# Adding up the squares of two norms on GpSimd instead of VectorE, in a two-layer transformer trunk

## The chip, the core and the metric

The kernel runs on one core of a Trainium2 chip. The core's engines work beside each other: TensorE (PE in the profile; its weight loads are PEld), VectorE (DVE), ScalarE (ACT), GpSimd (POOL) and SyncE (SP), which here only issues DMAs. Each engine takes its instructions in a fixed order, and semaphores hold an instruction until what it reads is there. The metric is the device time of one execution in microseconds (us). Three executions of the kernel before took 1200.5, 1200.5 and 1201.09 us; the median is 1200.5 us.

## What is computed

The reference runs two layers over 512 tokens of width 1024, in float32, with a memory of 256 tokens beside them:

```python
mem_n = rms_norm(mem, mem_norm_g)
for l in range(2):
    h = rms_norm(x, mix_norm_g[l])
    x = x + (mixer_attn_rglru(h, ...) if l == 0 else pool_mixer(h, od_pool_w[0], od_scale[0]))
    x = x + memory_xattn(rms_norm(x, xattn_norm_g[l]), mem_n, ...)
    x = x + sq_relu_mlp(rms_norm(x, mlp_norm_g[l]), mlp_w1[l], mlp_w2[l])
```

`rms_norm` multiplies x by `rsqrt(mean(x*x) + 1e-6)` and by a gain; the mean runs over the 1024 features of a token. `pool_mixer`, the mixer of the second layer, takes four groups of 256 features; for each it forms the mean over the last 2, 4, 8 or 16 tokens less the token itself, multiplies by a 256x256 matrix, scales, and the result is added to x. So two norms lie around the pooling mixer: the mixer's own norm, and the norm of the cross attention that follows it.

## The kernel before

**Layout.** x lies in SBUF transposed, as eight tiles of 128 features x 512 tokens (`self.x[0]` to `self.x[7]`; in the profile they are halves of the tiles x_85 to x_88). Tokens run along a row. A token's sum of squares is therefore a sum over eight tiles and then over 128 partitions. `square_tile` squares a tile on ScalarE into a fresh tile `sq` (the method A, line 264), and adds it to the first norm tile's `sq`, which is the accumulator (the method `tt`, line 274, on VectorE): seven adds of 128x512 for a norm. When all eight are in, `stats` lets TensorE form the column sums (line 379, tile misc), VectorE scales them (tile m_4 for the norm ahead of the mixer, m_5 for the one behind it), and GpSimd raises them to the power -1/2 (the method `G`, line 296, tile r). For the norm ahead of the mixer TensorE then spreads r over the partitions (line 677) and ScalarE stores it as R.

**Matmuls.** Each float32 operand is split into a high and a low part, and each product is three matmuls: high by high, high by low and low by high (`mm3`, line 366). A weight block arrives as a 512 KB tile `raw`; ScalarE writes its high part `wh`, and VectorE subtracts to get the low part `wl` (128x1024). The same split gives `xh` and `xl` for x times the gain of the norm.

**The stage around the change.** At the end of the first layer's MLP (`mlp(0, ...)`), VectorE adds the last results to x, and the squares of the mixer's norm follow. TensorE goes on with the first group of keys of the second layer's memory (`kv_group(1, 0, ...)`), then with the pooling matmuls, then with the other three groups of `kv_group`, and then with the queries of the cross attention, whose input is x after the mixer, as `xh` and `xl`. Beside these matmuls VectorE works through the pooling: for each of the eight x tiles `z` (matmul result times R, out of PSUM), window sums `zs` (for two groups a running sum `zc`), `df`, the update of x, and then `xl` and the add of the squares for the next norm.

**Order.** A planner in Python writes all engines' instruction lists. It keeps a model of the time at which each engine is free (`book`), lets each piece of work ask for an engine with a due time (the table `DUE`), and gives the engine to the earliest due among those whose inputs the model has ready. For an add on VectorE the model books 0.00104 us for each element of a row and 0.065 us more (0.60 us for 512). For an operation on GpSimd that is not a power it books `0.00215 * n + 0.2`, which is 1.30 us for 512. The chip then runs the lists in that order, whatever the real times are.

Of the kernel before, what the change touches and what calls it, by code (L numbers as in the profile page):

```python
# [9 lines left out]
ALU = mybir.AluOpType  # L10
# [16 lines left out]
V_MEM, V_MIX, V_XA, V_MLP = 0, 8, 24, 40  # L27
# [111 lines left out]
class Trunk:  # L139
# [422 lines left out]
                    self.tick()  # L562


    def new_norm(self, gcol, bc, forms=False, first=False):
        self.nid += 1
        return dict(first=first, id=self.nid, g=gcol, bc=bc, h=[None] * 8, l=[None] * 8, n=0, acc=None,
                    forms={} if forms else None)

    def norm_tile(self, N, k):  # L570
# [18 lines left out]
    def square_tile(self, N, k):  # L589
        sq = self.slot("sq")  # L590
        yield from self.A(sq, self.x[k], AF.Square)
        if N["acc"] is None:
            N["acc"] = sq
        else:
            yield from self.tt(N["acc"], N["acc"], sq, ALU.add)
        N["n"] += 1
        if N["n"] == 8:
            if N["first"]:
                self.spawn(self.stats(N), self.blk)
            else:  # L600
                self.spawn(self.stats(N), self.blk + DUE["stats"], DUE["stats_d"])
# [910 lines left out]
    def run(self):  # L1512
        self.start()
        self.mixer()
        kv0 = self.new_kv()
        for g in range(4):
            self.kv_group(0, g, kv0)
        n1 = self.new_norm(V_XA, False)
        self.gemm_t(self.y_op, lambda m, ps: self.update(m, ps, n1))
        n2 = self.new_norm(V_MLP, True, True)  # L1520
        self.xattn(0, n1, kv0, n2)
        n3 = self.new_norm(V_MIX + 8, True, first=True)
        self.mlp(0, n2, n3)
        kv1 = self.new_kv()
        self.kv_group(1, 0, kv1)
        n4 = self.new_norm(V_XA + 8, False)
        self.pool_mix(n3, n4)
        for g in range(1, 4):
            self.kv_group(1, g, kv1)
        n5 = self.new_norm(V_MLP + 8, True, True)  # L1530
        self.xattn(1, n4, kv1, n5)
        self.mlp(1, n5, None)
        self.drain()
# [77 lines left out]
```

## Time and profile before

| what | value |
|---|---|
| median of three executions | 1200.5 us |
| the profiled execution, its own time | 1200.98 us |
| its span on the core | 1199.2 us |
| TensorE busy | 1184.4 us |
| VectorE busy | 933.0 us |
| ScalarE busy | 668.5 us |
| GpSimd busy | 151.4 us |
| mean clock granted to TensorE | 0.998 of full speed |

The span runs from the first to the last instruction on the core; what the execution takes beyond it, 1.8 us here, lies around it. A busy TensorE is not a TensorE at its peak, since matmuls overlap: successive 512-column matmuls start about 0.23 us apart, though each is shown 0.39 us long. A wait is shown as the idle time in front of an instruction, with the instruction that ended it.

### The profile page before, as it was taken

The page shows a single profiled execution, that of the slowest core. Times are in us where ns is not written, and L with a number is a line of the kernel's source. Part 1 is how long each engine was busy: PE and PEld are TensorE (multiplying, and loading weights), DVE is VectorE, ACT ScalarE, POOL GpSimd, SP SyncE. Part 2 cuts the span into 40 slices and gives each one's busy share as a digit, 9 for nine tenths or more (in the row PEclk, how much of TensorE's full clock was granted, in tenths as well). Part 3 has the DMA queues.
Part 4 walks back from the last instruction along what each step waited for, and adds up shares of the span by engine and source line. Part 5 has one row for each costly group of instructions (what it writes and reads, how often), then busy time and mean ns, then how long its engine had stood idle before and what let it go on. Part 6 is the DMA issues. An engine that isn't in the chain of part 4 may idle for free.

```text
span 1199.2 us, 20004 instructions
## 1 busy us (share of the span) xinstructions
PE 1184.4 (99%) x7984; PEld 1091.8 (91%) x7984; DVE 933.0 (78%) x1419; ACT 668.5 (56%) x965; POOL 151.4 (13%) x180
## 2 busy tenths in 40 slices
PE   9999999999999999999999999999999999999998
PEld 6887888888889999999999987788899999999998
DVE  7959886555559977969969999856599779599697
ACT  6487774345456735646546657344477356465462
POOL 0110010010101121111112010001011211111110
PEclk9999999999999999999999999999999999999999
DMA  9233353322447699899899654424476998999984
GB/s 365 79 132 101 122 178 119 97 91 77 88 98 190 175 250 236 213 259 236 215 242 292 182 175 140 136 77 83 101 193 171 250 237 215 250 242 212 245 211 106
DMA packets 61293, 212.22 MB, mean 177 GB/s; under 512 B 6928, under 2 KB 7440, under 8 KB 61200
## 3 DMA queue, kind: packets, MB, share of 16 engines
q1 hardware_dynamic: 41472, 141.68, 33.9%
q0 software_dynamic: 19584, 69.21, 31.7%
q8 instruction: 62, 1.02, 0.3%
q14 instruction: 31, 0.25, 0.1%
q10 hardware_dynamic: 144, 0.05, 0.0%
HBM read 206.73 MB, written 4.19 MB: 176 GB/s over the span
## 4 chain that ended last, share of the span: by engine, by line
PE 89%; DVE 7%; ACT 2%; issue 1%; DMA 0%; SPq 0%; DVEq 0%; ACTq 0%
PE acc L366 55%; PE misc L366 32%; DVE wl L274 2%; PE misc L373 1%; PE misc L379 1%; DVE x L274 1%; DVE xl L274 0%; DVE p L274 0%; DVE fl L274 0%; DVE hs L274 0%; ACT a L264 0%; DVE zc L274 0%; DVE sq L274 0%; DVE zs L274 0%; DMA raw<-wpack 0%
## 5 line engine op out<-in xcount | busy, mean ns | idle before, releaser
L264 ACT ACTIVATE wh<-raw 128x1024 fp32r<-128x1024 f32 (+1 forms) x321 | 334.1, 1050 | 309.4 <-PE acc L366 130.0
L274 DVE TENSOR_TENSOR wl<-raw,wh 128x1024 fp32r<-128x1024 f32 (+1 forms) x321 | 387.5, 1213 | 136.8 <-ACT wh L264 133.2
L415 POOL DMA_DIRECT2D raw<-wpack x128 | 111.3, 872 | 627.7 <-DVE wl L274 320.4
L366 PE MATMUL misc<-fl,wh 128*128 128x256 f32 x448 | 127.0, 283 | 1.1 <-DVE fl L274 1.1
L366 PE MATMUL acc<-fl,wh 128*128 128x256 f32 x448 | 126.9, 283 | 0.5 <-DVE x L274 0.5
L366 PE MATMUL misc<-fh,wh 128*128 128x256 f32 x448 | 126.8, 283 | 0.0
L366 PE MATMUL misc<-fh,wl 128*128 128x256 f32 x448 | 126.8, 283 | 0.0
L366 PE MATMUL acc<-fh,wh 128*128 128x256 f32 x448 | 126.8, 283 | 0.0
L366 PE MATMUL acc<-fh,wl 128*128 128x256 f32 x448 | 126.8, 283 | 0.0
L366 PEld LDWEIGHTS misc<-fl,wh 128*128 128x128 f32 x448 | 86.0, 192 | 1.5 <-DVE fl L274 1.5
L366 PEld LDWEIGHTS acc<-fl,wh 128*128 128x128 f32 x448 | 86.0, 192 | 0.7 <-DVE x L274 0.7
L366 PEld LDWEIGHTS acc<-fh,wh 128*128 128x128 f32 x448 | 86.0, 192 | 0.0
L366 PEld LDWEIGHTS acc<-fh,wl 128*128 128x128 f32 x448 | 86.0, 192 | 0.0
L366 PEld LDWEIGHTS misc<-fh,wl 128*128 128x128 f32 x448 | 86.0, 192 | 0.0
L366 PEld LDWEIGHTS misc<-fh,wh 128*128 128x128 f32 x448 | 86.0, 192 | 0.0
L366 PE MATMUL acc<-xh,wh 128*128 128x512 f32 x208 | 82.7, 398 | 2.7 <-ACT xh L264 1.7
L366 PE MATMUL acc<-xl,wh 128*128 128x512 f32 x208 | 82.7, 398 | 0.9 <-DVE xl L274 0.8
L366 PE MATMUL acc<-xh,wl 128*128 128x512 f32 x208 | 82.2, 395 | 1.4 <-DVE wl L274 1.4
L366 PE MATMUL acc<-oh,wh 128*128 128x512 f32 x160 | 62.7, 392 | 0.7 <-ACT oh L264 0.7
L366 PE MATMUL acc<-oh,wl 128*128 128x512 f32 x160 | 62.8, 392 | 0.0
L366 PE MATMUL acc<-ol,wh 128*128 128x512 f32 x160 | 62.5, 391 | 0.2 <-DVE ol L274 0.2
L366 PE MATMUL acc<-wl,mh 128*128 128x512 f32 x128 | 50.7, 396 | 1.1 <-DVE wl L274 1.1
(290 smaller groups left out, 3217.5 us busy)
## 6 DMA issues: line engine op xcount, KB each, us to landing
raw<-wpack SPq DMA_DIRECT2D x253, 512.0 KB, 4.8
raw<-wpack POOLq DMA_DIRECT2D x128, 512.0 KB, 7.3
x<-xT SPq DMA_DIRECT2D x8, 256.0 KB, 5.1
outT<-x SPq DMA_DIRECT2D x6, 256.0 KB, 2.2
raw<-wpack SPq DMA_DIRECT2D x4, 256.0 KB, 4.6
memr<-memT SPq DMA_DIRECT2D x4, 256.0 KB, 3.7
spill<-mh SPq DMA_DIRECT2D x4, 256.0 KB, 2.0
spill<-ml SPq DMA_DIRECT2D x4, 256.0 KB, 2.2
```

What stands on the lines that cost most here:

```text
L264: self.nc.scalar.activation(out, in_, func, **kw)
L274: getattr(self.nc.vector, fn)(out, *args, **kw)
L366: self.nc.tensor.matmul(out, a, b, start=start and i == 0, stop=stop and i == 2, skip_group_check=shared)
L373: self.nc.tensor.transpose(out, in_, self.ident)
L379: self.nc.tensor.matmul(ps[:, t:t + 1], sq[:, t * 128:t * 128 + 128], self.one, start=True, stop=True)
L415: self.nc.gpsimd.dma_start(out=raw, in_=self.ins["wpack"][b], accum_op=ALU.add)
```

## The change

`new_norm` takes a flag `gp`. In a norm that has it, the seven adds of `square_tile` are issued on GpSimd (through `G`) instead of VectorE (through `tt`). The two norms around the pooling mixer get the flag: `n3` ahead of it and `n4` behind it. The squares stay on ScalarE, and the other four norms stay as they were.

```diff
--- before.py
+++ after.py
@@ -562,9 +562,9 @@
                     self.tick()
 
 
-    def new_norm(self, gcol, bc, forms=False, first=False):
+    def new_norm(self, gcol, bc, forms=False, first=False, gp=False):
         self.nid += 1
-        return dict(first=first, id=self.nid, g=gcol, bc=bc, h=[None] * 8, l=[None] * 8, n=0, acc=None,
+        return dict(first=first, gp=gp, id=self.nid, g=gcol, bc=bc, h=[None] * 8, l=[None] * 8, n=0, acc=None,
                     forms={} if forms else None)
 
     def norm_tile(self, N, k):
@@ -591,6 +591,8 @@
         yield from self.A(sq, self.x[k], AF.Square)
         if N["acc"] is None:
             N["acc"] = sq
+        elif N["gp"]:
+            yield from self.G(N["acc"], N["acc"], sq, ALU.add)
         else:
             yield from self.tt(N["acc"], N["acc"], sq, ALU.add)
         N["n"] += 1
@@ -1519,11 +1521,11 @@
         self.gemm_t(self.y_op, lambda m, ps: self.update(m, ps, n1))
         n2 = self.new_norm(V_MLP, True, True)
         self.xattn(0, n1, kv0, n2)
-        n3 = self.new_norm(V_MIX + 8, True, first=True)
+        n3 = self.new_norm(V_MIX + 8, True, first=True, gp=True)
         self.mlp(0, n2, n3)
         kv1 = self.new_kv()
         self.kv_group(1, 0, kv1)
-        n4 = self.new_norm(V_XA + 8, False)
+        n4 = self.new_norm(V_XA + 8, False, gp=True)
         self.pool_mix(n3, n4)
         for g in range(1, 4):
             self.kv_group(1, g, kv1)
```

Since the planner sees other bookings, it also writes some rows in another order. Three places are shown. First, VectorE at the end of the first layer's MLP, before (aN and acc are MLP results that are added to x; x_85 to x_88 hold x):

```order
L274 TENSOR_TENSOR x_88<-x_88,aN 128x2x256
L274 TENSOR_TENSOR sq<-sq 128x512
L274 TENSOR_TENSOR x_87<-x_87,aN 128x2x256
L274 TENSOR_TENSOR x_88<-x_88,aN 128x2x256
L274 TENSOR_TENSOR x_87<-acc_76,x_87 128x2x256
L274 TENSOR_TENSOR wl<-raw,wh 128x1024
L274 TENSOR_TENSOR sq<-sq 128x512 x2
L274 TENSOR_TENSOR x_86<-acc_77,x_86 128x2x256
L274 TENSOR_TENSOR x_88<-acc_78,x_88 128x2x256
L274 TENSOR_TENSOR wl<-raw,wh 128x1024
L274 TENSOR_TENSOR sq<-sq 128x512 x2
L274 TENSOR_TENSOR wl<-raw,wh 128x1024
```

and after the change:

```order
L274 TENSOR_TENSOR x_88<-x_88,aN 128x2x256
L274 TENSOR_TENSOR x_87<-x_87,aN 128x2x256
L274 TENSOR_TENSOR x_88<-x_88,aN 128x2x256
L274 TENSOR_TENSOR x_87<-acc_76,x_87 128x2x256
L274 TENSOR_TENSOR wl<-raw,wh 128x1024
L274 TENSOR_TENSOR x_86<-acc_77,x_86 128x2x256
L274 TENSOR_TENSOR x_88<-acc_78,x_88 128x2x256
L274 TENSOR_TENSOR wl<-raw,wh 128x1024 x3
L274 SCALAR_TENSOR_TENSOR xl<-x_85,vec,xh 128x512 x2
```

The adds `sq<-sq` are gone, seven of them up to the first `xl`; the three weight conversions `wl` now follow each other, and the rest keeps its order.

Second, VectorE at the end of the pooling, from the first `xl` of x_88 to the second, which is the last tile that the queries need. Before:

```order
L274 SCALAR_TENSOR_TENSOR xl<-x_88,vec,xh 128x512
L274 TENSOR_TENSOR zs<-zc 128x496
L274 TENSOR_TENSOR sq<-sq 128x512
L274 TENSOR_TENSOR zs<-zs,cst 128x16
L274 TENSOR_TENSOR wl<-raw,wh 128x1024
L274 SCALAR_TENSOR_TENSOR df<-zs,z 128x512
L274 TENSOR_TENSOR sq<-sq 128x512
L274 SCALAR_TENSOR_TENSOR x_88<-df,vec,x_88 128x512
L274 TENSOR_TENSOR wl<-raw,wh 128x1024
L274 SCALAR_TENSOR_TENSOR xl<-x_88,vec,xh 128x512
```

and after the change:

```order
L274 SCALAR_TENSOR_TENSOR xl<-x_88,vec,xh 128x512
L274 SCALAR_TENSOR_TENSOR zc<-cst,z 128x512
L274 TENSOR_TENSOR wl<-raw,wh 128x1024
L274 TENSOR_TENSOR zs<-zc 128x496
L274 TENSOR_TENSOR wl<-raw,wh 128x1024
L274 TENSOR_TENSOR zs<-zs,cst 128x16
L274 SCALAR_TENSOR_TENSOR df<-zs,z 128x512
L274 TENSOR_TENSOR wl<-raw,wh 128x1024
L274 SCALAR_TENSOR_TENSOR x_88<-df,vec,x_88 128x512
L274 SCALAR_TENSOR_TENSOR xl<-x_88,vec,xh 128x512
```

Two adds are gone here, and the running sum `zc` with the weight conversion behind it comes after the first `xl` instead of ahead of it. From the end of the MLP to this last `xl` VectorE has the same 29 weight conversions in both, and 12 instructions fewer after the change: the seven adds of n3 and five of n4. The other two adds of n4 stood behind this place.

Third, GpSimd's list between the MLP and the queries (r_4 and r_5 are the powers of the two norms, xrk those of the memory's keys, xqs those of the queries). Before:

```order
L415 DMA raw<-wpack 128x1024 x2
L296 TENSOR_TENSOR r_4_7327<-m_4_7326,cst 128x4
L296 TENSOR_TENSOR xrk<-xvv,cst 128x2 x4
L296 TENSOR_TENSOR r_5_8023<-m_5_8022,cst 128x4
L296 TENSOR_TENSOR xqs<-xqv,cst 128x4 x2
```

and after the change:

```order
L415 DMA raw<-wpack 128x1024 x2
L296 TENSOR_TENSOR sq<-sq 128x512 x7
L296 TENSOR_TENSOR r_4_7333<-m_4_7332,cst 128x4
L296 TENSOR_TENSOR xrk<-xvv,cst 128x2 x4
L296 TENSOR_TENSOR sq<-sq 128x512 x7
L296 TENSOR_TENSOR r_5_8008<-m_5_8007,cst 128x4
```

The seven adds of n3 stand in front of r_4 and of the xrk, and the seven of n4 in front of r_5. On TensorE the column sums of n3 move back by one matmul, and in the pooling the accumulator banks change places.

## Rows read from the trace of the kernel before

**Rows 1.** The page's part 1: busy microseconds, share of the span and instructions of each engine
```profile
PE 1184.4 (99%) x7984; PEld 1091.8 (91%) x7984; DVE 933.0 (78%) x1419; ACT 668.5 (56%) x965; POOL 151.4 (13%) x180
```

**Rows 2.** Windows, all engines: stretch, its length, busy (xinstructions), clock, DMA share, GB/s
```profile
680.00:690.00 10.00, 9.10 (x56) 7.68 (x56) 9.79 (x15) 9.30 (x16) 0.00 (x0) 1.00 0.40 118
...
735.00:745.00 10.00, 9.78 (x43) 7.77 (x42) 9.97 (x15) 6.13 (x10) 0.00 (x0) 1.00 0.43 147
...
755.00:766.00 11.00, 9.23 (x40) 7.08 (x38) 11.00 (x15) 4.72 (x7) 0.00 (x0) 1.00 0.53 181
767.00:771.00 4.00, 4.00 (x12) 3.19 (x11) 3.06 (x5) 2.35 (x4) 0.00 (x0) 0.59 0.73 247
```

**Rows 3.** Waits of PE, 670 to 800 us: total, times, longest
```profile
PE acc L366 <- DVE wl L274: 2.5, 4, 1.4
PE acc L366 <- ACT xh L264: 1.7, 1, 1.7
PE acc L366 <- DVE xl L274: 0.5, 1, 0.5
```

**Rows 4.** Timeline of PE, end of the pooling mixer: start, us, instruction, idle before
```profile
744.85 0.39 PE L366 MATMUL acc<-xh,wh 128*128 128x512 f32 x1
745.08 0.39 PE L366 MATMUL acc<-xl,wh 128*128 128x512 f32 x1
746.88 0.50 PE L366 MATMUL acc<-xh,wl 128*128 128x512 f32 x1 [1.42 <-DVE wl L274]
...
763.34 0.39 PE L366 MATMUL acc<-xh,wl 128*128 128x512 f32 x1
765.38 0.50 PE L366 MATMUL acc<-xh,wh 128*128 128x512 f32 x1 [1.66 <-ACT xh L264]
766.43 0.50 PE L366 MATMUL acc<-xl,wh 128*128 128x512 f32 x1 [0.54 <-DVE xl L274]
...
768.52 0.63 PE L366 MATMUL acc<-xh,wl 128*128 128x512 f32 x1
768.95 0.63 PE L366 MATMUL acc<-xh,wh 128*128 128x512 f32 x1
```

**Rows 5.** Timeline of DVE, in the same columns, around both norms
```profile
681.06 0.69 DVE L274 TENSOR_TENSOR sq<-sq 128x512 f32<-128x512 f32 x1
681.66 1.29 DVE L274 TENSOR_TENSOR x<-x,aN 128x512 f32<-128x512 f32 x2
...
687.19 1.22 DVE L274 TENSOR_TENSOR wl<-raw,wh 128x1024 fp32r<-128x1024 f32 x1
...
765.62 0.75 DVE L274 SCALAR_TENSOR_TENSOR xl<-x,vec,xh 128x512 fp32r<-128x512 f32 x1
```

**Rows 6.** The tile sq: form, count, duration ns min/median/max, first and last start
```profile
L274 DVE TENSOR_TENSOR sq<-sq x42: 681/684/694, 9.3 to 900.9; 128x512 f32<-128x512 f32 x42
```

**Rows 7.** Timeline of DVE, two weight conversions early in the program
```profile
149.68 1.22 DVE L274 TENSOR_TENSOR wl<-raw,wh 128x1024 fp32r<-128x1024 f32 x1
...
151.81 2.36 DVE L274 TENSOR_TENSOR wl<-raw,wh 128x1024 fp32r<-128x1024 f32 x2
```

**Rows 8.** Timeline of POOL (GpSimd), small powers of 128x2 values
```profile
142.52 0.69 POOL L296 TENSOR_TENSOR m_r<-m_m,cst 128x2 f32<-128x2 f32 x1 [26.84 <-DVE m_m L274]
...
149.94 1.52 POOL L296 TENSOR_TENSOR xrk<-xvv,cst 128x2 f32<-128x2 f32 x1 [6.42 <-DVE xvv L274]
152.06 1.52 POOL L296 TENSOR_TENSOR xrk<-xvv,cst 128x2 f32<-128x2 f32 x1 [0.61 <-DVE xvv L274]
```

**Rows 9.** Groups of POOL instructions by form: count, busy us, mean ns
```profile
L1081 POOL MEMSET pth<- 128x128 f32 x4 | 0.8, 204 | 51.7 <-PE acc L366 51.7
...
L1602 POOL MEMSET const-float32-0.0<- 128x1 f32 x1 | 0.1, 98 | 0.2 <-issue 0.2
```

**Rows 10.** Timeline of PE, column sums of the first norm
```profile
693.82 0.95 PE L379 MATMUL misc<-cst,sq 128*128 128x1 f32 x8
```

## The prediction

> **What bounds the kernel now.** I began with the busy times by engine: TensorE is busy for 1184.4 of 1199.2 us and GpSimd for 151.4 [rows 1]. So a change that leaves the matmuls alone can only act where TensorE waits, and GpSimd as a whole has room. Next I cut the stretch from the end of the MLP to the queries into windows, since a mean over the program says nothing of this stage. Here VectorE is the full engine: it is busy for 9.79 of 10 us at 680 to 690, 9.97 of 10 at 735 to 745, and 11.00 of 11 at 755 to 766 [rows 2]. The list of TensorE's waits for 670 to 800 us says what this costs: four waits for a `wl`, 2.5 us in all, one of 1.7 us for an `xh`, and one of 0.5 us for an `xl` [rows 3]. The timeline of TensorE shows them: 1.42 us at 746.88 for a weight conversion, then 1.66 us and 0.54 us at 765.38 and 766.43, where it wants the last `xh` and `xl` of x behind the pooling [rows 4]. The `xh` is ScalarE's, but its input is the update of x on VectorE. So in this stage the time is set by when VectorE gets to its last `xl`, at 765.62 [rows 5].
>
> The waits cost more than their idle time. After the one of 1.42 us the start of the next matmul lies 1.80 us behind the last, where 0.23 us is the usual step: 0.15 us more than the idle time [rows 4]. For six waits that is 0.9 us. And at 767 to 771 the granted clock is 0.59 of full speed [rows 2]; within that stretch matmuls start 0.43 us apart, the step at 1.2 GHz instead of 2.4 [rows 4], just behind the longest waits. Over 4 us that is 4 x 0.41 = 1.6 us. All in all VectorE's lateness costs 4.7 + 0.9 + 1.6 = 7.2 us here, and that is the most that the change can win.
>
> **What VectorE gains.** One add of squares takes 684 ns at the median [rows 6], but the next instruction starts 0.60 us after it (681.06 to 681.66) [rows 5], so an add removed is worth 0.60 us. Up to the last `xl` there are 12 fewer: 7.2 us. If that were all, VectorE would come 7.2 us earlier to where TensorE waited 2.2 us after having already lost some 3 us upstream, and nearly all of the 7.2 us lost would come back.
>
> **What GpSimd takes, and what it does to VectorE.** No row shows an add of 128x512 on GpSimd, so its time is bounded. From below: a write of 128 elements takes 204 ns and one of a single element 98 ns [rows 9], so 0.83 ns an element, and 512 elements of one stream take 0.43 us. From above: an add has two reads and a write, 1.28 us if all three go one after the other; nothing makes it cheaper than one stream. The small operations of the same kind need 0.69 us for two elements [rows 8], but these are powers, so a part of this is computing. With a start-up of some 0.2 us the planner's own booking of 1.30 us lies inside, and I take 1.3 us for an add.
>
> That would be harmless on an idle engine, were it not for how the two engines meet. A power of 128x2 takes GpSimd 0.69 us at 142.52, but 1.52 us at 149.94 and at 152.06 [rows 8]. In both of the latter VectorE was in the middle of a `wl`, a subtraction with both inputs in SBUF: one from 149.68 to 150.90, the other the first of two from 151.81, which ends at about 153.03 [rows 7]. GpSimd's instructions end at 151.46 and 153.58, both 0.55 us behind the end of that `wl`. So GpSimd did not get its inputs until VectorE's two-input instruction was over, and in the second case it got in between two that followed each other closely. The two engines exclude each other on such reads, and the order is by who comes first. If VectorE holds GpSimd up, an add that GpSimd has begun should hold up VectorE's next two-input instruction, for as long as it reads. These rows can't show that, since two elements are read in no time; 512 are not.
>
> The Trainium skill says so in "SBUF — State Buffer", section "Who interferes with whom": a VectorE instruction with two SBUF inputs contends with a GpSimd instruction that reads SBUF, and whichever begins second is blocked for the whole of the other. The trace agrees for the half in which GpSimd waits, with 1.52 against 0.69 us [rows 8]; the other half no row shows.
>
> How long such an add holds VectorE up: at least 0 (if it yields) and at most the 1.28 us of all three streams. Two reads over one way in are 0.86 us; I take the middle of 0.86 and 1.28, 1.07 us. Not every instruction of VectorE is hit: by the kernel's code `z`, `kTl`, `xvl` and the adds from acc have one input in PSUM, about 15% of its rows around the 14 adds. So an add costs VectorE about 0.85 x 1.07 = 0.91 us where it used to cost 0.60.
>
> "GPSIMD Engine Reference" in the Trainium skill, section "Elementwise — side-by-side cycle accounting", gives about 2.6 cycles an element at 1.2 GHz for a two-input add, an estimate of 1.11 us for 512; by that figure the sum below would be half a microsecond higher. No row here shows such an add.
>
> **The sum.** Before the last `xl` come the seven adds of n3 and about six of n4: the sixth follows the square of the first half of x_88, which is ready while VectorE has nine instructions to go. VectorE loses 13 x 0.91 = 11.8 us and gains 7.2 us: it comes to the last `xl` 4.6 us later. It is full throughout [rows 2], so nothing absorbs this, and TensorE waits so much longer at 746 and 765. The drop of the clock behind these waits stays, at about its 1.6 us. The seven adds of n4 cost nothing beyond this: r_5 is wanted only at the queries' sums.
>
> The adds of n3 have a second cost that I set at nothing. TensorE takes the column sums in its order, at 693.82 [rows 10]. The last four squares come together at about 687; four adds in a row, each behind a `wl` of VectorE (1.1 us) and then 1.1 us long, end at about 696, so TensorE would wait some 2 us there. VectorE works on meanwhile, and as its last `xl` sets the end of the stage, this wait only takes the place of a later one. If that cover failed, it would be 2 us more.
>
> From the profiled execution's 1200.98 us: 1205.6 us. The median of the runs is 0.5 us lower than that execution, so 1205.1 us.
>
> **The rivals.**
> - *VectorE isn't held up.* The exclusion works one way, or GpSimd yields. Then the 7.2 us come back, except for what the pipeline still loses: 1193.3 to 1196 us. For it: no row shows VectorE waiting for GpSimd. Against it: GpSimd's wait by itself shows that the reads share something, and that it got in between two adjacent `wl` shows that VectorE has no standing right of way.
> - *The hold is about as long as the add it replaces.* With 0.45 to 0.70 us for an add, VectorE comes out between 1.4 us earlier and 1.9 us later: 1199.1 to 1202.4 us. For it: the one-stream bound of 0.43 us, and that some of GpSimd's time is start-up, in which it need not hold anything. Against it: two reads and a write in 0.5 us would have to run beside each other.
> - *GpSimd starves.* VectorE's instructions overlap by some 0.08 us, so GpSimd might only get in at one with a single input. The four last adds of n3 would then begin when VectorE itself stops at m_4, which wants the sum: VectorE would lie idle for 4 x 1.3 = 5.2 us, of the 7.2 us 2 us are won: 1198.5 us. The entry at 153.03 speaks against it.
>
> **How the numbers follow.** This measurement can tell a difference of about 0.2%, 2.4 us, from none. The forecast, VectorE held up for longer than it saves, gets 0.58; with 0.8 to 1.25 us for an add its own range is 1203.7 to 1209.6 us. VectorE not held up gets 0.20, the even exchange 0.17, starving 0.05. The range from 1194.5 to 1210 us takes in the two-sided bound of the hold but for its extreme ends. Slower by over 0.2% (over 1202.9): 0.58. Within 0.2%: 0.17 for the even exchange. Faster (under 1198.1): 0.25, of the first and the last rival, which lies at the edge.
>
> **What would show it.** Right: the adds on GpSimd show 1.2 us and more, many over 2 us with a `wl` or `xl` of VectorE in front; VectorE's two-input instructions after 680 us have gaps or are lengthened by about 1 us, next to an add; the last `xl` ends near 771 us instead of 766.4; TensorE's waits in this stage grow from 4.7 to about 9 us, still behind `wl`, `xh` and `xl`. Wrong: VectorE's steps unchanged beside the adds and the last `xl` at about 759 us; or TensorE's longest wait at the column sums of n3, with VectorE idle ahead of m_4.

## The result, and the profile after

The kernel after the change takes 1208.84 us at the median of six executions (1208.28 to 1209.95), against 1200.5 us before: the ratio is 1.0074, with a 95% interval of 1.0063 to 1.0085. It is slower by 8.3 us. The profiled execution took 1208.91 us with a span of 1207.1 us; before it was 1200.98 and 1199.2 us.

The busy times by engine, which answer to [rows 1]:

```profile
PE 1185.7 (98%) x7984; PEld 1093.0 (91%) x7984; DVE 936.4 (78%) x1405; ACT 668.7 (55%) x965; POOL 182.8 (15%) x194
```

VectorE has 14 instructions fewer (1405 instead of 1419) and is nevertheless busy for 3.4 us longer, 936.4 us against 933.0. At 0.60 us each the 14 adds removed are worth 8.4 us, so its other instructions have become 11.8 us longer. The tile sq, form by form (count, duration in ns as min/median/max, first and last start), answers to [rows 6]:

```profile
L274 DVE TENSOR_TENSOR sq<-sq x28: 684/687/693, 9.2 to 908.9; 128x512 f32<-128x512 f32 x28
L296 POOL TENSOR_TENSOR sq<-sq x14: 1294/2075/3026, 680.6 to 774.4; 128x512 f32<-128x512 f32 x14
```

An add takes GpSimd 1.29 us at best and 2.08 us at the median. Where the time lies above 1.3 us it first waits. Three adds on GpSimd's timeline (start, us, instruction, idle time before it): the second begun as VectorE was about to run a tiny instruction, the first and the third while it was in two-input instructions of the pooling, with a weight conversion to come:

```profile
730.31 3.03 POOL L296 TENSOR_TENSOR sq<-sq 128x512 f32<-128x512 f32 x1
735.44 1.29 POOL L296 TENSOR_TENSOR sq<-sq 128x512 f32<-128x512 f32 x1 [2.11 <-ACT sq L264]
743.47 2.81 POOL L296 TENSOR_TENSOR sq<-sq 128x512 f32<-128x512 f32 x1 [6.73 <-ACT sq L264]
```

And VectorE's timeline in the same columns, with rows that answer to [rows 5]:

```profile
685.61 5.69 DVE L274 TENSOR_TENSOR wl<-raw,wh 128x1024 fp32r<-128x1024 f32 x3
691.22 3.46 DVE L274 SCALAR_TENSOR_TENSOR xl<-x,vec,xh 128x512 fp32r<-128x512 f32 x2
...
703.77 0.69 DVE L274 TENSOR_REDUCE xss<-ksq 128x2 f32<-128x512 f32 x1 [1.58 <-ACT ksq L264]
...
730.36 0.68 DVE L274 TENSOR_TENSOR zs<-z 128x511 f32<-128x511 f32 x1
730.96 1.21 DVE L274 TENSOR_TENSOR wl<-raw,wh 128x1024 fp32r<-128x1024 f32 x1
732.80 1.08 DVE L274 SCALAR_TENSOR_TENSOR xl<-x,vec,xh 128x512 fp32r<-128x512 f32 x1 [0.62 <-ACT xh L264]
...
735.60 1.16 DVE L274 TENSOR_TENSOR zs<-zs,cst 128x4 f32<-128x4 f32 x1
...
743.31 0.68 DVE L274 TENSOR_TENSOR zs<-zc 128x504 f32<-128x504 f32 x1
743.90 1.22 DVE L274 TENSOR_TENSOR wl<-raw,wh 128x1024 fp32r<-128x1024 f32 x1
745.03 1.27 DVE L274 TENSOR_TENSOR zs<-zs,cst 128x8 f32<-128x8 f32 x1
...
764.17 2.31 DVE L274 TENSOR_TENSOR_SCAN zc<-cst,z 128x512 f32<-128x512 f32 x1
...
772.79 0.75 DVE L274 SCALAR_TENSOR_TENSOR xl<-x,vec,xh 128x512 fp32r<-128x512 f32 x1 [0.79 <-ACT xh L264]
```

The tiny `zs<-zs,cst` of 128x4 at 735.60 should take 0.16 us; it took 1.16, up to 736.76, and the add that was running ended at 736.73. At 745.03 GpSimd waits first: the add began at 743.47, in the middle of a `zs`; the `wl` behind it still went ahead of the add, which ended at 746.28, 1.16 us after the end of that `wl` at 745.12; the tiny instruction behind the `wl` took 1.27 us and ended at 746.30. So GpSimd waits for VectorE's two-input instruction, and then VectorE's next one waits for GpSimd: ten times up to the last `xl` for 1.0 to 1.15 us, twice for less (0.51 us for a `wl` at 682.76, 0.34 us for the `xl` at 732.80). GpSimd doesn't get in at every boundary: four of the 14 adds (those begun at 680.58, 730.31, 743.47 and 750.81) let one or two more two-input instructions pass, and the one begun at 730.31 got in only behind the `wl` that ended at 732.17, where VectorE stood idle. What decides this at a boundary these traces don't show. Three `wl` in a row take 5.69 us instead of 3.5, two `xl` 3.46 instead of 1.40, and a running sum `zc` 2.31 instead of 1.22. The last `xl` of the pooling starts at 772.79 instead of 765.62 [rows 5]: 7.2 us later. The row at 703.77 shows VectorE idle for 1.58 us, the last one for 0.79 us.

TensorE's waits from 670 to 800 us (total, times, longest) answer to [rows 3]:

```profile
PE acc L366 <- ACT xh L264: 3.2, 1, 3.2
PE misc L379 <- POOL sq L296: 2.9, 1, 2.9
PE acc L366 <- DVE xvl L274: 2.0, 2, 1.6
PE acc L366 <- DVE wl L274: 1.2, 1, 1.2
PE misc L679 <- POOL r L296: 1.0, 1, 1.0
```

There are 10.3 us of them, 4.7 us before. The column sums of n3 wait 2.9 us for the last add on GpSimd, and the spreading of r another 1.0 us; the rest is again behind VectorE, or behind ScalarE's `xh`, which waits for VectorE's update of x. Windows of all engines, in the columns of [rows 2]:

```profile
680.00:690.00 10.00, 9.90 (x61) 8.66 (x60) 10.00 (x11) 9.76 (x15) 9.02 (x4) 1.00 0.47 159
695.00:700.00 5.00, 4.15 (x15) 3.02 (x15) 5.00 (x7) 0.60 (x1) 2.44 (x2) 0.68 0.31 104
755.00:766.00 11.00, 10.59 (x47) 8.44 (x46) 10.96 (x12) 3.67 (x6) 3.02 (x2) 1.00 0.30 94
...
773.00:778.00 5.00, 5.00 (x11) 3.56 (x12) 2.52 (x3) 2.99 (x5) 1.73 (x1) 0.50 0.56 197
778.00:780.00 2.00, 2.00 (x13) 1.78 (x12) 1.38 (x3) 0.59 (x2) 0.00 (x0) 0.81 0.01 2
```

In these windows VectorE is shown as full as before, but a part of its busy time is now the time for which it is held up. The granted clock is 0.50 at 773 to 778, just behind the wait of 3.2 us for `xh`, that is at 1.2 instead of 2.4 GHz for 5 us, and 0.81 over the next 2 us; before, it was 0.59 over 4 us [rows 2]. This costs 5 x 0.50 + 2 x 0.19 = 2.9 us instead of 1.6. There is another drop to 0.68 at 695 to 700, behind the wait at the column sums.

### The profile page after: what moved, and what is told of

Its sections match the earlier page's. It is cut to its first block, busy times and chain, and to the rows that moved or that the text cites. A ratio compares the mean times of both kernels' runs of the same rounds, so it can differ in the third digit from the quotient of the medians.

```text
span 1207.1 us, 20021 instructions
## 1 busy us (share of the span) xinstructions
PE 1185.7 (98%) x7984; PEld 1093.0 (91%) x7984; DVE 936.4 (78%) x1405; ACT 668.7 (55%) x965; POOL 182.8 (15%) x194
## 4 chain that ended last, share of the span: by engine, by line
PE 87%; DVE 8%; ACT 2%; issue 1%; POOL 0%; DMA 0%; SPq 0%; DVEq 0%; ACTq 0%
PE acc L366 53%; PE misc L366 32%; DVE wl L274 2%; PE misc L373 1%; PE misc L379 1%; DVE zs L274 1%; DVE xl L274 1%; DVE x L274 1%; DVE zc L274 0%; DVE p L274 0%; DVE fl L274 0%; DVE hs L274 0%; ACT a L264 0%; DMA raw<-wpack 0%; PE misc L679 0%
## 5 line engine op out<-in xcount | busy, mean ns | idle before, releaser
L366 PEld LDWEIGHTS acc<-xh,wh 128*128 128x128 f32 x208 | 39.8, 191 | 17.7 <-ACT xh L264 5.3
```

The lines of the kernel that those rows point to most:

```text
L366: self.nc.tensor.matmul(out, a, b, start=start and i == 0, stop=stop and i == 2, skip_group_check=shared)
```

## The experiments

The theory P is that of the prediction: an add on GpSimd and an instruction of VectorE with two inputs in SBUF exclude each other, and in this stretch VectorE has no time to give. Its rivals: the planner's new order costs the time (O), the late sums of n3 do (L), or any access of GpSimd to SBUF holds VectorE up (W).

**No adds at all.** The ceiling of what the change could win.

```diff
         elif N["gp"]:
-            yield from self.G(N["acc"], N["acc"], sq, ALU.add)
+            pass
```

> Left out: the fourteen adds of squares of the two norms; each norm's sum holds only its first tile. Everything else as after the change, in nearly the same order. Theory P (an add on GpSimd and a two-input instruction of VectorE exclude each other): VectorE is relieved of 12 x 0.60 = 7.2 us before its last xl of the pooling and nothing holds it up, so 1193.3 to 1195.5 us. Rival O (the planner's new order of instructions is what costs): the order is still the new one, so 1203 us and more. Rival L (the late sums of the first norm, on which TensorE waits in its order): the sums are not late any more, 1193 to 1196 us as well.

Measured: 1194.34 us, ratio 0.9951 (0.9936 to 0.9966) to 1199.66 us before on this chip: 5.3 us faster. Its engines:

```profile
PE 1181.1 (99%) x7984; PEld 1090.7 (91%) x7984; DVE 924.5 (78%) x1405; ACT 668.0 (56%) x965; POOL 151.6 (13%) x180
```

VectorE is busy for 8.5 us less than before, 0.61 us for each of the 14 adds, as worked out. The order isn't the cause (O falls). Of the 7.2 us some 2 us don't come back, and VectorE's timeline shows where they are:

```profile
696.62 0.69 DVE L274 TENSOR_REDUCE xss<-ksq 128x2 f32<-128x512 f32 x1 [1.50 <-ACT ksq L264]
...
760.55 0.75 DVE L274 SCALAR_TENSOR_TENSOR xl<-x,vec,xh 128x512 fp32r<-128x512 f32 x1 [0.79 <-ACT xh L264]
```

The last `xl` starts 5.1 us earlier than before. At 696.62 VectorE, relieved, waits 1.50 us for its input, where it waited 0.47 us before; and in this order it stands idle for 0.79 us ahead of its last `xl`, as in the kernel after the change. Against this run, the change lengthens VectorE's work by 936.4 - 924.5 = 11.9 us, 0.85 us for an add.

**GpSimd as busy, but without reading.** The planner books the two writes as it books an add.

```diff
         elif N["gp"]:
-            yield from self.G(N["acc"], N["acc"], sq, ALU.add)
+            yield ("pool", [sq])
+            for c in range(2):
+                self.nc.gpsimd.memset(sq, 0.0)
+            self.book("pool", 1.30, [sq], [sq])
```

> Left out as in the run without adds; in the place of each add GpSimd writes zeros over the squared tile, twice (two MEMSETs of 128x512, some 0.5 us each by 0.83 ns an element), so that it is about as busy, but reads nothing. Theory P, as a matter of reads: as without adds, 1193.3 to 1196 us, and no instruction of VectorE longer than before. Rival W (any access of GpSimd to SBUF holds VectorE up): 14 x 1 us x 0.85 more than without adds, some 1204 to 1207 us.

Measured: 1194.64 us, ratio 0.9953 (0.9938 to 0.9968), the same as without adds. The engines, and the tile sq in the columns above:

```profile
PE 1180.8 (99%) x7984; PEld 1090.3 (91%) x7984; DVE 925.0 (78%) x1405; ACT 667.9 (56%) x965; POOL 167.1 (14%) x208
```

```profile
L597 POOL MEMSET sq<- x28: 525/527/533, 681.0 to 762.0; 128x512 f32 x28
```

Twelve of the writes beside VectorE's three `wl` in a row, which took 5.69 us in the kernel after the change:

```profile
683.92 6.48 POOL L597 MEMSET sq<- 128x512 f32 x12 [1.86 <-ACT sq L264]
685.45 3.48 DVE L274 TENSOR_TENSOR wl<-raw,wh 128x1024 fp32r<-128x1024 f32 x3
```

28 writes of 128x512 of 0.53 us each lengthen VectorE's work by no more than 0.5 us in all (925.0 against 924.5). So a write alone doesn't collide, and W falls; what collides comes with the add's reading (a read without a write was not run). As GpSimd is busy here for 14.8 us (28 x 0.527), its being occupied costs nothing either.

**Adds on both engines.** The hold without the relief.

```diff
         elif N["gp"]:
-            yield from self.G(N["acc"], N["acc"], sq, ALU.add)
+            yield from self.tt(N["acc"], N["acc"], sq, ALU.add)
+            yield from self.G(sq, sq, sq, ALU.add)
```

> VectorE keeps its fourteen adds, and GpSimd does fourteen adds of the same size beside them (sq + sq into sq, which nobody uses). Nothing is left out. Theory P: no relief, and the hold alone: 12 to 14 adds x 0.85 to 0.95 us = 10 to 13 us more, 1210.5 to 1213.5 us. Rivals L and O: nobody waits for these adds and VectorE's list is that of before, so 1200 to 1202 us.

Measured: 1209.95 us, ratio 1.008 (1.0062 to 1.0097), 10.3 us slower, as much as was expected, though a little under the bounds given as times, since before took 1199.66 us on this chip. It is slower although nobody waits for what GpSimd computes:

```profile
PE 1186.9 (98%) x7984; PEld 1093.0 (90%) x7984; DVE 941.1 (78%) x1419; ACT 669.4 (55%) x965; POOL 175.4 (15%) x194
```

VectorE is busy for 8.1 us more than before with the same instructions. That is a little under 0.6 us an add instead of 0.85: these adds read one tile twice (the fastest took 1.04 us), and two of them fall behind the stretch. The last `xl` comes at 774.69, 9.1 us later than before. By this 10.3 us is more than VectorE's lengthening; the granted clock of 0.51 at 773 to 778 explains a part, as after the change. L, late sums on GpSimd, doesn't explain it: TensorE waits 1.2 us at the column sums here too, but for VectorE's own adds.

**One norm at a time.**

```diff
-        n4 = self.new_norm(V_XA + 8, False, gp=True)
+        n4 = self.new_norm(V_XA + 8, False)
```

> Only the norm ahead of the pooling mixer (n3) is added up on GpSimd; n4 is back on VectorE. Theory P: 7 x 0.84 = 5.8 us of hold, 7 x 0.60 = 4.2 us saved, and about 2.5 us of idle time of VectorE behind the late column sums: 4.1 us more, 1203.5 to 1206 us. Rival: the whole loss is in n4, then 1200 to 1201 us.

Measured: 1203.2 us, ratio 1.0025 (1.0016 to 1.0033) to 1200.37 us before: 2.8 us slower, just under the bounds given. TensorE's waits for the sums are there as after the change, and the last `xl` comes at 767.94:

```profile
PE misc L379 <- POOL sq L296: 2.9, 1, 2.9
...
PE misc L679 <- POOL r L296: 1.2, 1, 1.2
```

```profile
767.94 0.74 DVE L274 SCALAR_TENSOR_TENSOR xl<-x,vec,xh 128x512 fp32r<-128x512 f32 x1
```

```diff
-        n3 = self.new_norm(V_MIX + 8, True, first=True, gp=True)
+        n3 = self.new_norm(V_MIX + 8, True, first=True)
```

> Only the norm behind the pooling mixer (n4) is added up on GpSimd; n3 is back on VectorE. Theory P: 6 x 0.96 = 5.8 us of hold and 5 x 0.60 = 3.0 us saved before the last xl: 2.8 us more, 1202.5 to 1204.5 us, without a wait at the column sums of n3. Rival L (late sums of n3 are the whole loss): 1200.5 us or faster, as VectorE is relieved.

Measured: 1203.56 us, ratio 1.0031 (1.0019 to 1.0043): 3.2 us slower. No sum is late here. VectorE's `xl` at 753.88 takes 1.78 instead of 0.74 us, beside an add, and the last one comes at 769.19, 3.6 us later than before:

```profile
753.88 1.78 DVE L274 SCALAR_TENSOR_TENSOR xl<-x,vec,xh 128x512 fp32r<-128x512 f32 x1
...
769.19 0.74 DVE L274 SCALAR_TENSOR_TENSOR xl<-x,vec,xh 128x512 fp32r<-128x512 f32 x1
```

Each norm costs about 3 us. Together they cost 8.3, some 2 us more than the sum of the two. The last `xl` comes 2.3 and 3.6 us later with one norm each and 7.2 us with both, so 1.3 of the 2 us lie ahead of it; the idle times of VectorE ahead of an `xl` with both norms, 0.62 us at 732.80 and 0.79 us at 772.79, stand in neither of these two traces. Where the rest is from these runs don't say.

**The late sums planned for.**

```diff
-        self.book("pool", 0.63 if op == ALU.pow else 0.00215 * n + 0.2, [out], [a, b])
+        self.book("pool", 0.63 if op == ALU.pow else 2.08, [out], [a, b])
```

> As after the change, but the planner books 2.08 us (the median that the adds took) for an add on GpSimd instead of 1.30, so that the column sums of the first norm come later in TensorE's order. Theory P: the hold stays (11.6 us against 7.2 us saved), and the idle time of VectorE that the late sums bring, about 2.5 us, goes: 1204.5 to 1207 us. Rival L (the late sums are the whole loss): 1199 to 1202 us. If the wait at the sums only took the place of a later one, as the prediction had it: 1208 to 1209 us.

Measured: 1208.37 us (1207.01 to 1210.18), ratio 1.0069 (1.0051 to 1.0087): nothing won, and not the 1204.5 to 1207 us that P gave; it lies where a wait that only takes the place of another would put it. TensorE no longer waits at the column sums, but elsewhere:

```profile
PE acc L366 <- ACT xkn L264: 3.1, 1, 3.1
PE acc L366 <- ACT xh L264: 3.0, 1, 3.0
PE acc L366 <- DVE wl L274: 2.6, 3, 1.1
PE misc L373 <- ACT xkn L264: 0.6, 1, 0.6
```

It now waits 3.1 us for the scaled keys `xkn`, whose powers GpSimd computes when VectorE, held up, hands over their sums. So a wait at one place turned into another. VectorE's idle time from 678 us to its last `xl` is 3.7 us, much as after the change (3.8). Whether the late sums cost anything of their own is not settled by this run; L as the whole loss has fallen.

**The adds out of the full stretch.** If VectorE's fullness is what makes the adds costly, they should cost little where VectorE is half idle. First only n4, its adds placed behind the last `xl`:

```diff
         yield from self.A(sq, self.x[k], AF.Square)
+        if N["id"] == 5:
+            yield "n5.7"
```

> n4 alone on GpSimd, as in the run with n4 only, but its seven adds wait until the last xl of x is written, when VectorE is half idle. Theory P: the same engine and the same adds outside the full stretch: VectorE has five adds fewer ahead of its last xl and isn't held up there, so 3.0 us less than before, 1196.5 to 1199.5 us. If GpSimd's adds cost as such, wherever they stand: 1202.5 to 1204.5 us, as with n4 only.

Measured: 1204.88 us, ratio 1.0042 (1.0029 to 1.0054), outside both ranges: a miss. GpSimd's timeline shows why: its adds stand at the same times as with n4 alone (there at 753.59 and 764.61):

```profile
753.45 1.52 POOL L296 TENSOR_TENSOR sq<-sq 128x512 f32<-128x512 f32 x1 [6.49 <-ACT sq L264]
764.48 2.97 POOL L296 TENSOR_TENSOR sq<-sq 128x512 f32<-128x512 f32 x1 [9.50 <-ACT sq L264]
```

A later place in the list of an engine that has nothing else to do delays nothing; an add begins when its square is there. The line put the adds later in the plan only, and their sums later in TensorE's order. So in the next run the squares wait as well, on ScalarE, whose list is full:

```diff
+        if N["id"] == 5:
+            yield "n5.7"
         yield from self.A(sq, self.x[k], AF.Square)
```

> n4 alone on GpSimd, and now its squares on ScalarE too wait until the last xl of x is planned, so that the adds on GpSimd really come behind the full stretch (in the run before, GpSimd had nothing else to do and began each add as soon as its square was there, whatever its place in the list). Theory P: no hold ahead of VectorE's last xl and five adds fewer there: the last xl about 3 us earlier than before the change, no wait of TensorE above 1 us there, 1196.5 to 1199.5 us, unless the queries' sums come late. If an add on GpSimd costs as such, wherever it stands: 1202.5 to 1204.5 us.

Measured: 1198.97 us, ratio 0.9987 (0.9979 to 0.9996): 1.6 us faster than before the change, where the same adds on the same engine at their old place cost 3.2 us. The adds run from 765.22 on, the last `xl` of x comes at 763.45 instead of 765.62 [rows 5], and TensorE's waits shrink to 2.4 us:

```profile
765.22 4.04 POOL L296 TENSOR_TENSOR sq<-sq 128x512 f32<-128x512 f32 x3 [40.66 <-ACT sq L264]
771.09 7.46 POOL L296 TENSOR_TENSOR sq<-sq 128x512 f32<-128x512 f32 x4 [1.83 <-ACT sq L264]
```

```profile
763.45 0.74 DVE L274 SCALAR_TENSOR_TENSOR xl<-x,vec,xh 128x512 fp32r<-128x512 f32 x1
```

```profile
PE acc L366 <- DVE wl L274: 0.9, 2, 0.7
PE acc L366 <- ACT xh L264: 0.8, 1, 0.8
PE acc L366 <- DVE xl L274: 0.5, 1, 0.5
PE misc L379 <- POOL sq L296: 0.2, 1, 0.2
```

**The same with all adds on VectorE**, with late adds alone, and with late squares and adds:

> As before the change (all adds on VectorE), but the seven adds of n4 wait until the last xl of x is written. Theory P with VectorE's last xl as the end of the stage: five adds fewer ahead of it, 3.0 us less, and some of the clock's drop: 1196 to 1198.5 us, unless the queries' sums come late. Rival (the sums of n4 then hold up the softmax): 1200 us or more.

Measured: 1197.97 us, ratio 0.9981 (0.9972 to 0.999), 2.4 us faster than before the change. The last `xl` starts at 763.25, and TensorE's waits are 2.0 us:

```profile
763.25 0.74 DVE L274 SCALAR_TENSOR_TENSOR xl<-x,vec,xh 128x512 fp32r<-128x512 f32 x1
```

```profile
PE acc L366 <- DVE wl L274: 1.5, 4, 0.7
PE acc L366 <- DVE xl L274: 0.5, 1, 0.5
```

> The same order as in the run with late squares on GpSimd, but all adds on VectorE: its control, and a rival to the version with late adds. Theory P: as late adds on VectorE, 1196.5 to 1199 us; within 1 us of the run with late squares on GpSimd, since VectorE is half idle there and has room either for the adds or for being held up.

Measured: 1197.73 us, ratio 0.9981 (0.9971 to 0.9991) to 1200.54 us before, as the run above. It is 1.2 us faster than the same order with the adds on GpSimd, a little over the 1 us expected; the two intervals overlap, so a small cost of the late adds on GpSimd is neither shown nor ruled out. Both beat the kernels before and after, without GpSimd: what helped is that five adds no longer stand ahead of the last `xl`.

## Why the prediction came out as it did

- *VectorE bounds the stage, and its last `xl` sets the end.* Right. With the last `xl` 7.2 us later the kernel is 8.3 us slower, and with it 2.4 us earlier (late adds on VectorE) it is 2.4 us faster. In the kernel after and the ten of the experiments, the shift of the last `xl` in the trace and the change of the median agree within 1.3 us: 5.1 us earlier goes with 5.3 us faster (no adds), 9.1 us later with 10.3 us slower (adds on both).
- *What VectorE gains, 0.60 us an add.* Right: 8.5 us of busy time for 14 adds.
- *An add on GpSimd takes about 1.3 us.* Right: 1.29 us undisturbed. The estimate of 1.11 us for 512 elements from the figure in "GPSIMD Engine Reference" of the Trainium skill (section "Elementwise — side-by-side cycle accounting") is less than the whole add; it lies within the 1.0 to 1.15 us for which an instruction of VectorE was held up.
- *VectorE is held up, by 0.91 us an add, 11.8 us in all.* This was the step that rested on an inference, as the rows before showed only GpSimd waiting. It was right: the lengthened rows up to the last `xl` add up to 11.6 us, 0.89 us for each of the 13 adds there, and all 14 cost 11.9 us of busy time. That it is so close is in part luck, since 1.07 us was the middle between two bounds that no row told apart. "Who interferes with whom" in "SBUF — State Buffer" of the Trainium skill agrees with both halves of this, GpSimd waiting and VectorE waiting, and the writes alone, 0.5 us in 28, agree with its limit to instructions that read.
- *The sum, 4.6 us later at the last `xl`.* Too small: 7.2 us. Hold less relief is 11.6 - 7.2 = 4.4 us. The other 2.8 us are idle time of VectorE, which the prediction set at nothing ("it is full throughout"). One part is the step "the adds of n3 have a second cost that I set at nothing": the wait at the column sums came, with 2.9 us, about as worked out, but the cover failed. VectorE doesn't simply work on: it ran out of input behind TensorE, 1.58 us at 703.77 and 0.27 us at 708.52, where it was 0.47 us before. (What this part would be worth without the late sums stays open, as the run that planned for them only moved the wait.) The second is the planner's order: the update of x_88 now stands right in front of its `xl`, with nothing for VectorE to do while ScalarE makes `xh` (0.79 us at 772.79, and the same without any adds). The order rows had shown this, and I read them only for their count. The third, 0.62 us at 732.80, is an `xh` that came late because ScalarE first waited 0.96 us for GpSimd's `xrk`; this power took 1.83 us from 728.50, beside a `wl`.
- *The drop of the clock stays at 1.6 us.* Too small: 2.9 us. These 1.3 us more and the 7.2 us, less the 0.5 us for which TensorE no longer waits for the last `xl` [rows 3], make 8.0 of the 8.3 us.
- *The rivals.* VectorE is held up, so the first falls; the hold of 0.85 us is longer than the 0.60 us saved, so the second falls; ten of the 14 adds held up a two-input instruction of VectorE by 1.0 us and more, and VectorE wasn't idle ahead of m_4, so the third falls. Something of it is there all the same: four adds let VectorE's next two-input instruction pass, and the one begun at 730.31 got in only when VectorE stood idle.

## What to carry to other kernels

Work moved from a full engine to an idle one relieves the full one only if the two don't share what they read through: before moving two-input work from VectorE to GpSimd, look in the trace for small GpSimd operations that last longer beside two-input instructions of VectorE, and count the hold (here 0.85 us for 128x512) against the relief (0.60 us). Where an engine bounds a stage, ask first which of its instructions needn't stand ahead of the one that sets the end: moving five adds behind it won 2.4 us without another engine. And a place in a list delays an instruction only on an engine that has something ahead of it to do.

## What had not been expected of the hardware

A VectorE instruction of 0.16 us can last 1.27 us, as at 745.03, when it starts behind GpSimd's reading, and in the profile this shows as its duration, not as a wait: no row names GpSimd as the releaser. Writes of 128x512 by GpSimd at 0.53 us each ran beside VectorE's two-input instructions and lengthened its work by no more than 0.5 us for 28 of them. And GpSimd, once it waits, doesn't always come next: the add begun at 743.47 in the middle of a `zs` had to let the whole `wl` behind that `zs` pass.
